# Gates of the first 128 tokens scattered into a table in DRAM and read back by row

## The chip, the core and the metric

One core of a Trainium2 chip. The time is the device time of one execution in microseconds; several runs give a median. One more execution was recorded by the profiler, and its own time stands beside its span.

## The reference

A block with gated, attention and memory branches and a feed-forward is followed by a second block with a state-space mixer, a convolution branch and a layer of experts, all in fp32 for 256 tokens of 1024 features. The change lies in the layer of experts: 16384 experts, numbered (i, j) with i and j below 128. Each token has 8 heads, and each head picks 16 experts with a softmax gate. Cut to that:

```python
q1, q2 = jnp.split(q, 2, axis=-1)                      # 8 heads
s1 = jnp.einsum("thd,hkd->thk", q1, sub_keys_1)
s2 = jnp.einsum("thd,hkd->thk", q2, sub_keys_2)
v1, i1 = lax.top_k(s1, 16); v2, i2 = lax.top_k(s2, 16)
cand = (v1[..., :, None] + v2[..., None, :]).reshape(t, 8, 256)
cand_idx = (i1[..., :, None] * 128 + i2[..., None, :]).reshape(t, 8, 256)
top_s, pos = lax.top_k(cand, 16)
expert_idx = jnp.take_along_axis(cand_idx, pos, axis=-1)
gate = jax.nn.softmax(top_s, axis=-1)
act = gelu(einsum("td,thkd->thk", x, w_down[expert_idx])) * gate
y = einsum("thk,thkd->td", act, w_up[expert_idx])
```

Different heads of one token can pick the same expert; its gates then add.

## The kernel before

The kernel computes every expert for every token and makes the choice a multiplication with a table of gates that is zero nearly everywhere. `AT` holds, on partition j, for each i (128 rows) and each of the 256 tokens, first the activation and then its product with the gate.

Fp32 weights are split into a coarse and a fine fp32r half by `load_split` (lines 210 to 216): SP loads `wf` (four buffers), ScalarE casts it to `wh`, VectorE subtracts to get `wl` (three buffers each). A product is then three matmuls (`mm3`, lines 220 to 222).

In the order of the program:

- First block, with its feed-forward in the loop `for g in range(9)` (weights `w_ff1` and `w_ff2`, matmuls into `ff` and the output banks). GpSimd's queue has one memset and one small operation there.
- Second block's mixer. Then queries (`w_q`) and scores.
- `select(t)`, once for each half of the tokens, finds the experts on VectorE (top 16 in lines 1291 to 1297, positions and softmax to 1338) and leaves i, j and gate in `sl`, token on the partition, one column for each of the 8 x 16 choices. Three transposes (line 1342) and a copy (line 1343) turn them into `jt`, one column a token, a part of the buffer `small`.
- Down projection: loop over pairs of i, 128 weight tiles `wd`, each 24 matmuls into `S` (lines 220 to 222). Gelu brings a pair into `AT` (lines 1440, 1443), and the tokens whose gates are there already are multiplied in on the way (line 1444).
- `gates()`, beside the down projection, in 64 blocks of four tokens: `og` (VectorE, line 1407) is the one-hot of i times the gate, `oh` (ScalarE, lines 1409 and 1410) the one-hot of j, and for each token one product of the two (line 1414) gives the 128x128 table of its gates in `pg`. Rows of `AT` that are there are multiplied by it (line 1418), the others get it as a first value (line 1421).
- Up projection: loop over i. A row of `AT` is split into `ah` (ScalarE, line 346) and `al` (VectorE, line 347), the weights `wu` into `wh` and `wl`, and 12 matmuls add into `acc` (line 1470). `ah` and `al` have two buffers up to row 96 and four after it.
- The end: norm and output.

Selection and gates are generators in a list of background work (`Background`). After each weight tile `bg.run` takes steps from it until the tile's budget is used: `BUDGET["select"]` up to the first block of gates, `BUDGET["down"]` from there. A step's cost is what it yields (a block of gates 1.1 + 0.5).

That is the order in which the program is traced. A planner then orders each engine's queue: among the instructions whose inputs and buffers are ready by its own clock, that which was traced first goes first. Only what is pinned (`pin`) keeps its place. On the chip every queue runs in the order it was given, each instruction waiting for its semaphores; SP's and GpSimd's DMAs too.

Of the kernel before, what the change touches and what calls it, by code (L numbers as in the profile page):

```python
# [7 lines left out]
F32 = mybir.dt.float32  # L8
F32R = mybir.dt.float32r
I32 = mybir.dt.int32  # L10
U32 = mybir.dt.uint32
AF = mybir.ActivationFunctionType
OP = mybir.AluOpType
AX = mybir.AxisListType
PSUM = bass.MemoryType.PSUM

P = 128
T = 256
# [17 lines left out]
for _n, _w in _ROWS:  # L36
# [8 lines left out]
BUDGET = dict(  # L45
    qk=1.5, kv=7.03, u=2.75, wo=2.51, diag=2.05,
    conf_c=0.995, xbc_c=1.4, conv=1.0,
    z=3.3, z_b=0.867, dt_wait=0.0575, ln_wait=6.66, wo2=3.32, wo2_b=5.58, gn_b=0.1,
    q=0.772, q_b=1.27, select=1.21, down=1.87,
)  # L50
FFN_WAIT, MIX_WAIT = 4.5, 5.5

# [104 lines left out]
def tile_two_blocks(ctx: ExitStack, tc: tile.TileContext, A, out):  # L157
    nc = tc.nc
    bg = Background()
# [7 lines left out]
    def bank(name):  # L167
        return ppool.tile([P, 512], F32, tag="bank", name=name)

    cst = cpool.tile([P, NCST], F32, name="cst")  # L170
    ident = cst[:, 0:P]
# [3 lines left out]
    iota = cst[:, 4 * P:5 * P]  # L175
# [9 lines left out]
    rows = cpool.tile([P, NROW], F32, name="rows")  # L185
# [144 lines left out]
    def pin(ins):  # L330
        tc.keep_in_program_order(ins)
# [55 lines left out]
    resid = sres.enter_context(tc.tile_pool(name="resid", bufs=1))  # L387
# [6 lines left out]
    ap = s1a.enter_context(tc.tile_pool(name="ap", bufs=1))  # L394
# [62 lines left out]
    for t in range(2):  # L457
        r = rc1[:, t:t + 1]
# [345 lines left out]
    def activations(g, bs):  # L804
# [7 lines left out]
            split_to(ah[:, 2 * i:2 * i + 2, :], al[:, 2 * i:2 * i + 2, :], a)  # L812
        held.append((ah, al))

    for g in range(9):
        if g < 8:
            bs, outs = pair_banks(4, f"ff1_{g}")
            if g == 0:

                pb = outs2[5][0]  # L820
                ch.add(stats_steps(fp, x1, "ffn", rbf, eps1, where=(outs2[7][0], [pb[:, 0:P], pb[:, P:T]]), wait=FFN_WAIT))
            proj_fm(A["w_ff1"][:, :, g * 512:(g + 1) * 512], 8, 4, h2h, h2l, outs, chain=1.0)
            if g == 0:
                first_bs = bs
                continue
            if g == 1:
                ch.drain()
                activations(0, first_bs)
            activations(g, bs)
        if g == 1:  # L830
            ch.add(meta_steps())
            bg.add(tap_blocks())
        if g >= 1:
            ah, al = held[g - 1]
            for j in range(4):
                k = (g - 1) * 4 + j
                wh, wl = load_split(A["w_ff2"][:, k, :], [P, 1024])
                for m, (o, fb) in enumerate(outs2):
                    c = slice(m * P, (m + 1) * P)
                    mm3(o, wh[:, c], wl[:, c], ah[:, j, :], al[:, j, :], k == 0 and fb, k == 31)  # L840
                ch.run(1.0)
                bg.run(BUDGET["diag"])
# [456 lines left out]

    ready = dict(q=0)  # L1300

    def select(t):
        for h in range(8):
            while ready["q"] < h // 2 + 1:
                yield None
            for s in range(2):
                yield from top16(V[:, h, s, :], Ix[:, h, s, :], sc[t][:, 2 * h + s, :], tk[s])
            cand = cands[h % 2]
            pin(nc.vector.tensor_add(cand, V[:, h, 0, :].unsqueeze(2).to_broadcast([P, 16, 16]),
                                 V[:, h, 1, :].unsqueeze(1).to_broadcast([P, 16, 16])))  # L1310
            yield 0.4
            yield from top16(ts[:, h, :], pos[:, h, :], cand.rearrange("p a b -> p (a b)"), tk2[h % 2])
        while ready["q"] < 8:
            yield None

        pin(nc.vector.tensor_scalar(ab[:, 0], pos, 4, None, op0=OP.logical_shift_right))
        nc.vector.tensor_scalar(ab[:, 1], pos, 15, None, op0=OP.bitwise_and)
        nc.vector.tensor_copy(abf, ab)
        nc.vector.tensor_copy(If, Ix)
        yield 1.0  # L1320
        for s in range(2):
            for q in range(2):
                hs = slice(4 * q, 4 * q + 4)
                e3 = eq.rearrange("p h j a -> p (h j) a")
                pin(nc.vector.tensor_tensor(e3, abf[:, s, hs].rearrange("p h j -> p (h j)").unsqueeze(2).to_broadcast([P, 64, 16]),
                                        iota[:, 0:16].unsqueeze(1).to_broadcast([P, 64, 16]), op=OP.is_equal))
                yield 1.2
                for h in range(4):
                    pin(nc.vector.tensor_mul(eq[:, h], eq[:, h], If[:, 4 * q + h, s, :].unsqueeze(1).to_broadcast([P, 16, 16])))
                    yield 0.4  # L1330
                pin(nc.vector.reduce_sum(sl[:, s, 64 * q:64 * q + 64], e3, axis=AX.X))
                yield 1.2
        g3 = sl[:, 2, :].rearrange("p (h j) -> p h j", h=8)
        nc.vector.tensor_sub(g3, ts, ts[:, :, 0:1].to_broadcast([P, 8, 16]))
        nc.scalar.activation(g3, g3, AF.Exp)
        nc.vector.reduce_sum(zs, g3, axis=AX.X)
        nc.vector.reciprocal(zs, zs)
        nc.vector.tensor_mul(g3, g3, zs.unsqueeze(2).to_broadcast([P, 8, 16]))
        yield 0.8
        pj = bank(f"pj{t}")  # L1340
        for i in range(3):
            nc.tensor.transpose(pj[:, i * P:(i + 1) * P], sl[:, i, :], ident)
        nc.scalar.copy(jt[:, :, t * P:(t + 1) * P], pj[:, :384].rearrange("p (i c) -> p i c", i=3))
        yield 0.2
# [31 lines left out]
    sq1.close()  # L1376
    small = resid.tile([P, 8 * T], F32, name="small", tag="x2")
    jt = small[:, 0:3 * T].rearrange("p (i t) -> p i t", i=3)
    ready["q"] = 8
    stage = [small[:, 3 * T + i * 512:3 * T + (i + 1) * 512] for i in range(2)]  # L1380

# [3 lines left out]
    atp = sat.enter_context(tc.tile_pool(name="atp", bufs=1))  # L1385
    AT0 = atp.tile([P, NA, T], F32, name="AT0")
    parts = [(0, NA, AT0)]
    state = dict(rows=0, toks=0)

    def at_rows(a, b):  # L1390
        for lo, hi, t in parts:
# [4 lines left out]
    NB = 4  # L1396

    def gates():
        t = p1.tile([P, P - NA, T], F32, tag="at1", name="AT1")
        parts.append((NA, P, t))  # L1400
        for b in range(T // NB):
            t0 = b * NB
            oh = gp.tile([P, NB, P], F32, tag="oh", name=f"oh{b}")
            og = gp.tile([P, NB, P], F32, tag="og", name=f"og{b}")
            for i in range(NB):
                c = t0 + i
                nc.vector.tensor_scalar(og[:, i, :], iota, jt[:, 0, c:c + 1], jt[:, 2, c:c + 1], op0=OP.is_equal, op1=OP.mult)  # L1407

                nc.scalar.activation(oh[:, i, :], iota, AF.Abs, scale=-1.0, bias=jt[:, 1, c:c + 1])  # L1409
            nc.scalar.activation(oh, oh, AF.Relu, scale=-1.0, bias=1.0)  # L1410
            yield 1.1
            pg = bank(f"pg{b}").rearrange("p (t i) -> p t i", t=NB)
            for i in range(NB):
                nc.tensor.matmul(pg[:, i, :], oh[:, i, :], og[:, i, :], start=True, stop=True, skip_group_check=True)  # L1414
            n = state["rows"]
            for a, e, r in at_rows(0, n):
                r = r[:, :, t0:t0 + NB]
                nc.vector.tensor_mul(r, r, pg.rearrange("p t i -> p i t")[:, a:e, :])
            for a, e, r in at_rows(n, P):
                r = r[:, :, t0:t0 + NB]  # L1420
                nc.scalar.copy(r, pg.rearrange("p t i -> p i t")[:, a:e, :])
            state["toks"] = t0 + NB
            yield 0.5
# [4 lines left out]
    for i in range(0, P, 2):  # L1428
        S = bank(f"S{i}").rearrange("p (a t) -> p a t", a=2)
        for e in range(2):  # L1430
            wh, wl = load_split(A["wd"][i + e], [P, 8, P])
            for k in range(8):
                mm3(S[:, e, :], wh[:, k, :], wl[:, k, :], xth[:, k, :], xtl[:, k, :], k == 0 and e == 0, k == 7)
            bg.run(BUDGET["select"] if state["toks"] == 0 else BUDGET["down"])
        n = state["toks"]
        rs = list(at_rows(i, i + 2)) if len(parts) > 1 or i < NA else []
        assert len(rs) == 1
        r = rs[0][2]
        if n < T:
            nc.scalar.activation(r[:, :, n:], S[:, :, n:], AF.Gelu)  # L1440
        if n > 0:
            g = stage[(i // 2) % 2].rearrange("p (a t) -> p a t", a=2)
            nc.scalar.activation(g[:, :, :n], S[:, :, :n], AF.Gelu)
            nc.vector.tensor_mul(r[:, :, :n], r[:, :, :n], g[:, :, :n])
        state["rows"] = i + 2
    bg.drain()

# [3 lines left out]
    late = []  # L1451
    up = gp
    pin(nc.scalar.activation(first, first, AF.Sqrt))
    for i in range(P):
        (_, _, r), = list(at_rows(i, i + 1))
        r = r[:, 0, :]
        if i == NA:

            sat.close()
            up = sp.enter_context(tc.tile_pool(name="up", bufs=4))  # L1460
# [126 lines left out]
```

## Time and profile before

| | us |
|---|---|
| median of 3 runs | 1412.07 |
| lowest and highest | 1408.16, 1412.43 |
| the profiled execution's own time | 1407.69 |
| its span | 1406.0 |
| TensorE busy | 1384.8 (98%) |
| VectorE busy | 1013.7 (72%) |
| ScalarE busy | 814.5 (58%) |
| GpSimd busy | 43.0 (3%) |

The span goes from the first to the last instruction; the own time has 1.7 us around it. TensorE's matmuls are pipelined and their recorded ends are modelled, so that what one costs is read from the chain, where the pieces don't overlap, or from a count in a stretch. The granted clock over the span is 0.997 of full speed. Of a GpSimd DMA the trace shows the time that the engine takes to issue it, and separately the time to landing.

### The profile page before, as it was taken

The numbers are of one execution on the slowest core, as the hardware profiler recorded it, in microseconds if no ns is written. First come the engines' busy times: TensorE is split into PE (matmuls) and PEld (weight loads), VectorE is DVE, ScalarE is ACT, GpSimd is POOL, SyncE is SP. The second block draws the span as 40 slices with busy tenths as digits, with TensorE's granted clock in tenths as the row PEclk, the third lists the DMA queues.
The fourth block names the chain that finished last, engine by engine and source line by source line (L and its number), as shares of the span: only waits on it lengthen the run. The fifth ranks groups of instructions, "written<-read, shape, count | busy, mean of one in ns | idle before, by whom it ended". The sixth has DMA issues, their size and how long they took to land.

```text
span 1406.0 us, 26360 instructions
## 1 busy us (share of the span) xinstructions
PE 1384.8 (98%) x10313; PEld 1279.2 (91%) x10313; DVE 1013.7 (72%) x1966; ACT 814.5 (58%) x1431; POOL 43.0 (3%) x64
## 2 busy tenths in 40 slices
PE   9999999999999999999999999999999999999998
PEld 8988999999889899999999999999998888888886
DVE  6886875647557975889799867788875555555654
ACT  6565443435345764645454569999975555555554
POOL 2300000000310000000000000000000000000000
PEclk9999999999999999999999999999999999999999
DMA  8532665654743335446555544444455566656553
GB/s 273 167 91 94 193 194 193 186 175 137 223 137 113 113 121 181 150 150 188 188 180 187 189 165 136 135 136 136 135 172 188 186 188 188 188 192 184 191 185 116
DMA packets 84109, 233.64 MB, mean 166 GB/s; under 512 B 8816, under 2 KB 17904, under 8 KB 83856
## 3 DMA queue, kind: packets, MB, share of 16 engines
q1 hardware_dynamic: 82112, 228.46, 51.4%
q0 software_dynamic: 1296, 2.92, 0.8%
q8 instruction: 81, 1.33, 0.4%
q10 hardware_dynamic: 576, 0.57, 0.1%
q14 instruction: 44, 0.36, 0.1%
HBM read 226.22 MB, written 1.05 MB: 162 GB/s over the span
## 4 chain that ended last, share of the span: by engine, by line
PE 92%; DVE 3%; ACT 2%; DMA 1%; issue 1%; POOL 0%; SPq 0%; ACTq 0%; DVEq 0%
PE acc L1470 25%; PE S L222 9%; PE S L221 9%; PE S L220 9%; PE pg L1414 4%; PE ff L222 4%; PE ff L221 4%; PE ff L220 4%; PE cv L884 2%; PE wo L220 2%; PE wo L222 1%; PE wo L221 1%; PE cf L220 1%; PE q L221 1%; PE cf L222 1%; PE cf L221 1%
## 5 line engine op out<-in xcount | busy, mean ns | idle before, releaser
L216 DVE TENSOR_TENSOR wl<-wf,wh 128x1024 fp32r<-128x1024 f32 (+1 forms) x425 | 515.8, 1215 | 206.1 <-ACT wh L215 205.9
L215 ACT CAST wh<-wf 128x1024 fp32r<-128x1024 f32 (+1 forms) x425 | 441.8, 1040 | 316.1 <-PE S L221 114.6
L220 PE MATMUL S<-xth,wh 128*128 128x256 f32 x1024 | 291.4, 285 | 0.0
L221 PE MATMUL S<-xtl,wh 128*128 128x256 f32 x1024 | 288.4, 282 | 0.0
L222 PE MATMUL S<-xth,wl 128*128 128x256 f32 x1024 | 288.1, 281 | 0.0
L222 PEld LDWEIGHTS S<-xth,wl 128*128 128x128 f32 x1024 | 194.0, 189 | 0.0
L220 PEld LDWEIGHTS S<-xth,wh 128*128 128x128 f32 x1024 | 193.6, 189 | 0.0
L221 PEld LDWEIGHTS S<-xtl,wh 128*128 128x128 f32 x1024 | 192.4, 188 | 0.0
L1470 PE MATMUL acc<-wh,al 128*128 128x512 f32 x512 | 161.4, 395 | 0.0
L1470 PE MATMUL acc<-wl,ah 128*128 128x512 f32 x512 | 161.4, 395 | 0.0
L1470 PE MATMUL acc<-wh,ah 128*128 128x512 f32 x512 | 161.3, 395 | 0.0
L346 ACT CAST ah<-AT 128x256 fp32r<-128x256 f32 x128 | 51.8, 407 | 157.0 <-DVE wl L216 121.1
L1470 PEld LDWEIGHTS acc<-wh,al 128*128 128x128 f32 x512 | 96.0, 187 | 23.5
L1470 PEld LDWEIGHTS acc<-wl,ah 128*128 128x128 f32 x512 | 96.0, 187 | 23.5
L1470 PEld LDWEIGHTS acc<-wh,ah 128*128 128x128 f32 x512 | 95.9, 187 | 23.3
L347 DVE TENSOR_TENSOR al<-AT,ah 128x256 fp32r<-128x256 f32 x128 | 54.1, 425 | 68.7 <-PE acc L1470 67.9
L1409 ACT ACTIVATE oh<-cst,small 128x128 f32<-128x128 f32 x256 | 87.6, 402 | 0.0
L220 PE MATMUL ff<-h2h,wh 128*128 128x256 f32 x256 | 72.0, 282 | 2.3 <-ACT wh L215 2.0
L1407 DVE TENSOR_SCALAR og<-cst,small 128x128 f32<-128x128 f32 x256 | 73.9, 342 | 0.0
L221 PE MATMUL ff<-h2l,wh 128*128 128x256 f32 x256 | 71.6, 280 | 0.1
L222 PE MATMUL ff<-h2h,wl 128*128 128x256 f32 x256 | 70.9, 280 | 0.7 <-DVE wl L216 0.7
L221 PE MATMUL ff<-fal,wh 128*128 128x256 f32 x256 | 71.3, 280 | 0.0
(482 smaller groups left out, 2699.7 us busy)
## 6 DMA issues: line engine op xcount, KB each, us to landing
wf<-in_wd_dram SPq DMA_DIRECT2D x128, 512.0 KB, 3.5
wf<-in_wu_dram SPq DMA_DIRECT2D x128, 512.0 KB, 4.3
wf<-in_w_ff_dram SPq DMA_DIRECT2D x64, 512.0 KB, 3.5
wf<-in_w_out_dram SPq DMA_DIRECT2D x24, 512.0 KB, 3.5
wf<-in_w_conf_dram SPq DMA_DIRECT2D x16, 512.0 KB, 3.9
wf<-in_w_xbc_dram SPq DMA_DIRECT2D x16, 512.0 KB, 3.9
wf<-in_w_q_dram SPq DMA_DIRECT2D x16, 512.0 KB, 3.7
wf<-in_w_fm_dram SPq DMA_DIRECT2D x8, 512.0 KB, 4.7
```

The lines of the kernel that those rows point to most:

```text
L215: nc.scalar.copy(wh[:, :n], wf[:, :n])
L216: nc.vector.tensor_sub(wl[:, :n], wf[:, :n], wh[:, :n])
L220: nc.tensor.matmul(o, lh, rh, start=start, stop=False, skip_group_check=True)
L221: nc.tensor.matmul(o, lh, rl, start=False, stop=False, skip_group_check=True)
L222: nc.tensor.matmul(o, ll, rh, start=False, stop=stop, skip_group_check=True)
L346: nc.scalar.copy(dh, src)
L347: nc.vector.tensor_sub(dl, src, dh)
L884: nc.tensor.matmul(pcv[32 * g:32 * g + 32, i, :], taps[:, m, g, q, :], r4[:, i, g, 4 * q:4 * q + T], start=(i == 0 and q == 0), stop=(q == ...
L1407: nc.vector.tensor_scalar(og[:, i, :], iota, jt[:, 0, c:c + 1], jt[:, 2, c:c + 1], op0=OP.is_equal, op1=OP.mult)
L1409: nc.scalar.activation(oh[:, i, :], iota, AF.Abs, scale=-1.0, bias=jt[:, 1, c:c + 1])
L1414: nc.tensor.matmul(pg[:, i, :], oh[:, i, :], og[:, i, :], start=True, stop=True, skip_group_check=True)
L1470: nc.tensor.matmul(acc[t][f], l[:, c], w[:, f * 512:(f + 1) * 512], start=False, stop=e, skip_group_check=True)
```

## The change

For tokens 0 to 127 the one-hot products go. Instead:

- A table `G0` of 128 x 128 x 128 fp32 (8 MB) in DRAM is cleared by eight GpSimd DMAs from a tile of zeros, traced one by one in the feed-forward loop of the first block.
- `select(0)` ends in `scatter`: three VectorE operations make the address (i x 128 + j) x 128 + token, and for each of the 128 choices one indirect DMA on GpSimd adds 128 gates, one a token, to the table. The sixteen DMAs of a head are declared free of each other; a head's DMAs wait for those of the head before.
- `gates()` treats only tokens 128 to 255 (32 blocks), and the budget of the down projection goes from 1.87 to 1.05.
- In the down projection tokens 0 to 127 get only Gelu; in the up projection SP loads their gates by rows (three rows, then four at a time, into two parts of `small`, the first into the place of `jt`), and VectorE multiplies each row's 128 first tokens before the split.

```diff
@@ -46,7 +46,7 @@
     qk=1.5, kv=7.03, u=2.75, wo=2.51, diag=2.05,
     conf_c=0.995, xbc_c=1.4, conv=1.0,
     z=3.3, z_b=0.867, dt_wait=0.0575, ln_wait=6.66, wo2=3.32, wo2_b=5.58, gn_b=0.1,
-    q=0.772, q_b=1.27, select=1.21, down=1.87,
+    q=0.772, q_b=1.27, select=1.21, down=1.05,
 )
 FFN_WAIT, MIX_WAIT = 4.5, 5.5
 
@@ -812,7 +812,16 @@
             split_to(ah[:, 2 * i:2 * i + 2, :], al[:, 2 * i:2 * i + 2, :], a)
         held.append((ah, al))
 
+
+    G0 = tc.dram_tile([P * P * P, 1], F32, name="G0")
+    G0z = G0.rearrange("(p c n) o -> p c (n o)", p=P, c=8)
+    zg = dg.tile([P, 512], F32, name="zg")
+    nc.gpsimd.memset(zg, 0.0)
+
     for g in range(9):
+        if g >= 1:
+            nc.gpsimd.dma_start(G0z[:, g - 1, :].rearrange("p (a n) -> p a n", a=4),
+                                zg.unsqueeze(1).to_broadcast([P, 4, 512]))
         if g < 8:
             bs, outs = pair_banks(4, f"ff1_{g}")
             if g == 0:
@@ -1299,6 +1308,22 @@
 
     ready = dict(q=0)
 
+    def scatter(sl):
+
+        e, gv = idx.bitcast(F32), gates0
+        nc.vector.scalar_tensor_tensor(e, sl[:, 0, :], float(P), sl[:, 1, :], op0=OP.mult, op1=OP.add)
+        nc.vector.tensor_scalar(idx, e, float(P), tokc, op0=OP.mult, op1=OP.add)
+        nc.vector.tensor_copy(gv, sl[:, 2, :])
+        for h in range(8):
+            key = f"head{h}"
+            for j in range(16):
+                c = 16 * h + j
+                s = nc.gpsimd.indirect_dma_start(
+                    out=G0, out_offset=bass.IndirectOffsetOnAxis(ap=idx[:, c:c + 1], axis=0),
+                    in_=gv[:, c:c + 1], in_offset=None, compute_op=OP.add)
+                tc.declare_no_dep(s.ins, group=key, reason="the experts of a head differ")
+                tc.add_to_no_dep_group(key, s.ins)
+
     def select(t):
         for h in range(8):
             while ready["q"] < h // 2 + 1:
@@ -1337,6 +1362,9 @@
         nc.vector.reciprocal(zs, zs)
         nc.vector.tensor_mul(g3, g3, zs.unsqueeze(2).to_broadcast([P, 8, 16]))
         yield 0.8
+        if t == 0:
+            scatter(sl)
+            return
         pj = bank(f"pj{t}")
         for i in range(3):
             nc.tensor.transpose(pj[:, i * P:(i + 1) * P], sl[:, i, :], ident)
@@ -1376,6 +1404,11 @@
     sq1.close()
     small = resid.tile([P, 8 * T], F32, name="small", tag="x2")
     jt = small[:, 0:3 * T].rearrange("p (i t) -> p i t", i=3)
+    idx = small[:, 7 * T:7 * T + P].bitcast(U32)
+    gates0 = small[:, 7 * T + P:8 * T]
+    tokc = resid.tile([P, 1], F32, name="tokc", tag="tokc")
+    nc.vector.tensor_mul(idx.bitcast(F32), ident, iota)
+    nc.vector.reduce_sum(tokc, idx.bitcast(F32), axis=AX.X)
     ready["q"] = 8
     stage = [small[:, 3 * T + i * 512:3 * T + (i + 1) * 512] for i in range(2)]
 
@@ -1385,7 +1418,7 @@
     atp = sat.enter_context(tc.tile_pool(name="atp", bufs=1))
     AT0 = atp.tile([P, NA, T], F32, name="AT0")
     parts = [(0, NA, AT0)]
-    state = dict(rows=0, toks=0)
+    state = dict(rows=0, toks=P)
 
     def at_rows(a, b):
         for lo, hi, t in parts:
@@ -1398,8 +1431,8 @@
     def gates():
         t = p1.tile([P, P - NA, T], F32, tag="at1", name="AT1")
         parts.append((NA, P, t))
-        for b in range(T // NB):
-            t0 = b * NB
+        for b in range(P // NB):
+            t0 = P + b * NB
             oh = gp.tile([P, NB, P], F32, tag="oh", name=f"oh{b}")
             og = gp.tile([P, NB, P], F32, tag="og", name=f"og{b}")
             for i in range(NB):
@@ -1431,17 +1464,20 @@
             wh, wl = load_split(A["wd"][i + e], [P, 8, P])
             for k in range(8):
                 mm3(S[:, e, :], wh[:, k, :], wl[:, k, :], xth[:, k, :], xtl[:, k, :], k == 0 and e == 0, k == 7)
-            bg.run(BUDGET["select"] if state["toks"] == 0 else BUDGET["down"])
+            bg.run(BUDGET["select"] if state["toks"] == P else BUDGET["down"])
         n = state["toks"]
         rs = list(at_rows(i, i + 2)) if len(parts) > 1 or i < NA else []
         assert len(rs) == 1
         r = rs[0][2]
-        if n < T:
-            nc.scalar.activation(r[:, :, n:], S[:, :, n:], AF.Gelu)
-        if n > 0:
+        if n == P:
+            nc.scalar.activation(r, S, AF.Gelu)
+        else:
+            nc.scalar.activation(r[:, :, :P], S[:, :, :P], AF.Gelu)
+            if n < T:
+                nc.scalar.activation(r[:, :, n:], S[:, :, n:], AF.Gelu)
             g = stage[(i // 2) % 2].rearrange("p (a t) -> p a t", a=2)
-            nc.scalar.activation(g[:, :, :n], S[:, :, :n], AF.Gelu)
-            nc.vector.tensor_mul(r[:, :, :n], r[:, :, :n], g[:, :, :n])
+            nc.scalar.activation(g[:, :, P:n], S[:, :, P:n], AF.Gelu)
+            nc.vector.tensor_mul(r[:, :, P:n], r[:, :, P:n], g[:, :, P:n])
         state["rows"] = i + 2
     bg.drain()
 
@@ -1451,9 +1487,18 @@
     late = []
     up = gp
     pin(nc.scalar.activation(first, first, AF.Sqrt))
+    G0r = G0.rearrange("(i j t) o -> j i (t o)", i=P, j=P)
+
+    gts = {i: small[:, 512 * (i // 4 % 2):512 * (i // 4 % 2) + 512].rearrange("p (a t) -> p a t", a=4)
+           for i in range(3, P, 4)}
+    gts[0] = jt[:, :, 0:P]
     for i in range(P):
         (_, _, r), = list(at_rows(i, i + 1))
         r = r[:, 0, :]
+        if i in gts:
+            n0, gt = i, gts[i][:, :min(P - i, gts[i].shape[1]), :]
+            nc.sync.dma_start(gt, G0r[:, i:i + gt.shape[1], :])
+        nc.vector.tensor_mul(r[:, :P], r[:, :P], gt[:, i - n0, :])
         if i == NA:
 
             sat.close()
```

## Rows read from the trace of the kernel before

**Rows 1.** Page: busy shares of the engines, shares of the chain

```profile
PE 1384.8 (98%) x10313; PEld 1279.2 (91%) x10313; DVE 1013.7 (72%) x1966; ACT 814.5 (58%) x1431; POOL 43.0 (3%) x64
...
PE 92%; DVE 3%; ACT 2%; DMA 1%; issue 1%; POOL 0%; SPq 0%; ACTq 0%; DVEq 0%
```

**Rows 2.** Stretches, all engines: us, busy us (count), granted clock, DMA share, GB/s

```profile
138.00:146.00 8.00, 8.00 (x69) 8.00 (x69) 6.18 (x11) 2.48 (x5) 0.00 (x0) 1.00 0.27 61
146.00:154.00 8.00, 6.33 (x51) 5.93 (x51) 4.84 (x7) 3.72 (x6) 0.00 (x0) 1.00 0.90 313
240.00:260.00 20.00, 20.00 (x173) 20.00 (x172) 12.12 (x13) 8.57 (x9) 0.00 (x0) 1.00 0.59 185
706.00:826.00 120.00, 120.00 (x1017) 120.00 (x1016) 107.07 (x267) 61.36 (x78) 0.00 (x0) 1.00 0.58 185
826.00:1042.00 216.00, 216.00 (x1855) 216.00 (x1855) 176.24 (x431) 197.26 (x516) 0.00 (x0) 1.00 0.43 138
1042.00:1400.00 358.00, 358.00 (x1536) 287.53 (x1534) 210.55 (x258) 187.38 (x263) 0.00 (x0) 1.00 0.58 182
```

**Rows 3.** Chain that ended last, from 820 us: start us, us, what

```profile
825.42 0.33 PE pj L1342 x3
...
828.60 0.89 PE pg L1414 x8
```

**Rows 4.** Instructions of one tile or line: count, ns, first and last start

```profile
L1414 PE MATMUL pg<-og,oh x512: 270/275/275, 828.4 to 1038.9; 128*128 128x128 f32 x171
...
L1342 PE MATMUL pj<-cst,scr x6: 272/273/273, 705.6 to 825.5; 128*128 128x128 f32 x6
...
L1343 ACT COPY small<-pj x2: 467/467/467, 706.7 to 826.3; 128x384 f32<-128x384 f32 x2
```

**Rows 5.** Groups of VectorE, 700 to 826 and 826 to 1042 us

```profile
L1338 DVE TENSOR_TENSOR scr<-scr 128x128 f32<-128x128 f32 x1 | 0.3, 292 | 0.0
...
L1407 DVE TENSOR_SCALAR og<-cst,small 128x128 f32<-128x128 f32 x248 | 71.3, 342 | 0.0
```

**Rows 6.** DMA issues: engine, count, KB each, median us to landing

```profile
r<-h POOLq DMA_DIRECT2D x32, 71.0 KB, 3.3
...
m<-in_memT_dram SPq DMA_DIRECT2D x4, 256.0 KB, 5.4
...
out_dram<-res SPq DMA_DIRECT2D x4, 256.0 KB, 2.2
...
ws<-in_wsT_dram POOLq DMA_DIRECT2D x1, 384.0 KB, 7.0
```

**Rows 7.** Groups of GpSimd: count, busy us, mean ns of one

```profile
L873 POOL DMA_DIRECT2D r<-h x32 | 16.9, 537 | 36.8 <-PE cv L884 29.2 <-DVE sg L913 7.6
...
L602 POOL DMA_DIRECT2D bsb<-in_bs_dram x6 | 3.3, 564 | 0.0
...
L273 POOL TENSOR_TENSOR rc_y<-sd_y,cst 128x4 f32<-128x4 f32 x2 | 2.0, 1009 | 70.8 <-ACT sd_y L271 70.8
...
L273 POOL TENSOR_TENSOR rc_mem<-sd_mem,cst 128x2 f32<-128x2 f32 x1 | 0.7, 695 | 2.9 <-ACT sd_mem L271 2.9
```

**Rows 8.** Timelines of GpSimd and VectorE from 351 us: start us, us

```profile
351.40 8.49 POOL L873 DMA_DIRECT2D r<-h  x16 [7.63 <-DVE sg L913]
...
352.66 1.20 DVE L216 TENSOR_TENSOR wl<-wf,wh 128x1024 fp32r<-128x1024 f32 x1
```

**Rows 9.** Timelines of VectorE and ScalarE in one period of the up projection

```profile
1201.66 0.42 DVE L347 TENSOR_TENSOR al<-AT,ah 128x256 fp32r<-128x256 f32 x1 [0.56 <-PE acc L1470]
1202.67 1.23 DVE L216 TENSOR_TENSOR wl<-wf,wh 128x1024 fp32r<-128x1024 f32 x1 [0.58 <-ACT wh L215]
...
1201.13 0.41 ACT L346 CAST ah<-AT 128x256 fp32r<-128x256 f32 x1 [1.29 <-DVE wl L216]
1201.59 1.05 ACT L215 CAST wh<-wf 128x1024 fp32r<-128x1024 f32 x1
```

**Rows 10.** Timeline of VectorE at 708 us

```profile
708.28 0.33 DVE L1407 TENSOR_SCALAR og<-cst,small 128x128 f32<-128x128 f32 x1
```

## What the change does to the time: the prediction

> **What bounds the kernel now.** I read the page's busy shares first, then the chain that ended last, then a table of stretches by stage. TensorE is busy 98% of the span and makes 92% of the chain [rows 1]. The stretches [rows 2] show it without a gap from 706 to 1400 us at the full granted clock (1.00), through the stages that the change touches: the second selection beside the down projection (to 826), one-hot gates beside it (826 to 1042), up projection (1042 to 1400). VectorE is busy 107.07 of 120 us, 176.24 of 216 and 210.55 of 358 there, and the DMA engines 0.58, 0.43 and 0.58. So TensorE work taken out of these stages shortens the span, as long as nothing else comes last.
>
> **Removed: half of the one-hot products.** In the chain, the eight matmul records of one block of four tokens take 0.89 us [rows 3]. The 512 records [rows 4] are 64 blocks, 57.0 us. Half go: 32 x 0.89 = 28.5 us, all on the path. The three transposes of the first tokens go too, 0.33 us [rows 3]. ScalarE and VectorE lose half of their one-hot work, which lies beside TensorE and is worth nothing itself. Gain: 28.8 us.
>
> **Added: clearing the table.** Eight GpSimd DMAs of 1 MB (8.39 MB, pieces of 2 KB) in the first feed-forward. Two stretches price a piece. From 138 to 146 us only the 992-byte pieces of `raw` move: 0.27 x 16 engines x 8 us = 34.6 us for 61 GB/s x 8 us = 488 KB, 492 pieces, 70 ns each. From 146 to 154 it is 4 KB pieces of weights: 115 us for 2.50 MB, 611 pieces, 188 ns [rows 2]. The line through both, an estimate, is 32 ns plus 0.038 ns a byte: 110 ns for 2 KB, 52 for 512 B, 32 for 4 B. Clearing is 4096 x 110 ns / 16 = 28 us of all engines. The stage draws 185 GB/s at share 0.59 and the engines reach 313 [rows 2], so, spread out, it costs nothing. Nothing in it waits on the loop, however, and the planner puts ready work far ahead (below), so it may come in one burst near 146 us, when loads are catching up and TensorE already misses 1.7 us of 8 [rows 2]. With half of the engines the loads get 157 GB/s of the 185 wanted for 8.39 MB / 157 GB/s = 53 us: 1.5 MB short, 8 us, less what the four `wf` buffers (2 MB) hold. Bounds 0 and 8 us; I take 2.
>
> **Added: the scatter.** 128 indirect DMAs of 128 four-byte pieces on GpSimd, which has nothing else to do then [rows 2]. It can start when the first selection is through: its transposes start at 705.6 us [rows 4], and three small VectorE operations of about 0.29 us [rows 5] make the indices, so about 709. It must end before the up projection reads the table. Without the 28.8 us TensorE gets there at 1013 instead of 1042; the first load of gates takes 2.2 to 5.4 us (256 KB [rows 6]) and the multiply and split about 1 us, so the scatter has until about 1006. Each head's first DMA waits for the previous head's sixteen: seven landings at 3.3 us (the GpSimd DMA of `r` [rows 6]) are 23 us. That leaves (1006 - 709 - 23) / 128 = 2.14 us for each DMA. No row shows an indirect DMA. From below: a plain one takes GpSimd 0.54 to 0.56 us [rows 7]. From above: issue to landing one after another, 3.3 us (7.0 for the slowest GpSimd DMA, `ws` [rows 6]). I take 1.2: the plain DMA, which also writes 128 pieces for `bsb`, plus one of GpSimd's small arithmetic instructions (0.69 to 1.01 us [rows 7]) for fetching 128 offsets, since plain DMAs issued back to back don't wait for each other's landing (16 in 8.49 us [rows 8]). Then it ends at 709 + 154 + 23 = 886 us, 120 us early, hidden behind the down projection. On the DMA engines it is 16384 x 32 ns / 16 = 33 us; if adding makes a piece four times as dear, 131 us over these 300, which with 0.43 to 0.58 just fills them.
>
> **Moved: the budget.** The gates of the other tokens now get 1.05 a tile instead of 1.87: 32 blocks x 1.6 / 1.05 = 49 tiles after the second selection (826.3 us [rows 4]). A tile is 24 matmuls at 120 us / 1017 = 118 ns [rows 2], 2.83 us; with 28.5 us of products this ends at about 993, 20 us before the down projection does. The buffer of the first gate load (the old `jt`) is free then. So the scatter, not the gates, sets this load's time.
>
> **Added: gates in the up projection.** 33 loads on SP's queue ahead of weight loads, 8.39 MB in 512-byte pieces: 16384 x 52 ns / 16 = 53 us over 358, share 0.58 to 0.73, hidden. The second load overwrites rows 0 and 1 of the first and waits for their multiplies; the weight loads behind it wait too. That can cost a period once (0 to 3 us; I take 1). Later loads find their buffer free by the time SP gets there. The 128 multiplies of 128x128 cost VectorE 0.29 us each (its nearest row [rows 5]); per row it is busy 1.23 + 0.42 us of a period of 2.80 [rows 9], so 1.94 with them. The period is TensorE's: 358 us / 128 rows = 2.80, and VectorE waits 0.56 us for `acc` each time [rows 9].
>
> **Sum.** Span 1406.0, own time 1407.69: 1407.69 - 28.8 + 2 + 1 = 1381.9. The median shown, 1412.07, is 4.4 above this execution, so the same sum from the median is 1386. I forecast 1383, in a case of 1375 to 1390.
>
> **Rival 1, the scatter is late (ends slower).** One mechanism: GpSimd's time for each indirect DMA. Up to 2.14 us it is hidden; at 2.37 (the 29 us gone) the change is worth nothing; at 3.3, the landing row, it ends at 709 + 422 + 23 = 1154, 148 us late: 1531. Typical of it is 2.6: 709 + 333 + 23 = 1065, 59 late, 1442. For it: no row shows such an instruction, and the sixteen of a head must land in memory. Against: back-to-back issue at 0.53. Chance 0.17, of which 0.04 stays faster or equal.
>
> **Rival 2, VectorE keeps GpSimd from building descriptors.** If GpSimd worked only while VectorE is idle, it would have 12.9 us to 826 and 39.8 us after it [rows 2], plus the removed one-hots (128 x 0.342 = 43.8 [rows 5]) and about 20 us of the halved table multiplies, less the 29 us by which the stage is shorter: 87 us for 154 us of work. It ends 67 us into an idle up projection instead of 7 before it: 1383 + 60, about 1443. Against it: at 351 us GpSimd issued 16 DMAs in 8.49 us while VectorE ran operations nearly end to end, `wl` at 1.20 [rows 8]. For it: the og operations are of another kind than those, and an indirect DMA also reads its offsets. Chance 0.08. [...]
>
> **Rival 3, crowded DMA engines.** Adding pieces at over four times 32 ns, or the clearing in one burst, starve the weight loads: 5 to 30 us lost, 1388 to 1412. Chance 0.08.
>
> **Rival 4, a ring between VectorE and ScalarE.** If the multiply of the next row stands behind `wl` of this one, then `ah` waits for it, `wh` for `ah`, `wl` for `wh`: 1.23 + 0.29 + 0.03 + 0.46 + 1.08 = 3.09 us a row [rows 5, 9] against 2.80, 37 us in 128 rows: 1420. Against it: the planner fills gaps with whatever is ready; og of the first block ran at 708.28 us between selection steps, 120 us ahead of its products at 828.4 [rows 4, 10], and the multiplies are ready four rows ahead. Chance 0.07.
>
> **How the numbers follow.** Forecast 0.60, rivals 0.17, 0.08, 0.08, 0.07. The range, 1375 to 1425, holds the forecast, rivals 3 and 4 and the near end of rival 1; some 0.18 lie outside. About 0.3% (4 us) is what a measurement can tell from no change. Faster: 0.60, plus 0.07 of rival 3, 0.04 of rivals 1 and 2: 0.71. Same: 0.04. Slower: 0.25.
>
> **What would show it.** TensorE without gaps from 706 us on, 256 records of products, the up projection starting near 1013 + 2 us: right. [...] Gaps in TensorE near 150 us show the clearing. Most likely to be wrong is the 1.2 us.

## The result, and the profile after

The changed kernel takes 1574.02 us (median of 4 runs, 1572.73 to 1575.61) against 1410.53 for the kernel before: 1.1161 times as long, 95% interval 1.1137 to 1.1184. Forecast were 1383 us and a gain. The profiled execution has a span of 1571.0 us, 165.0 more than before.

The page, first its slices of 39 us. The rows are the engines' busy tenths, the granted clock, and the DMA engines' share:

```profile
PE   8997899999999999999900004999999999999998
...
DVE  6875766666478769898800004766676876666665
...
POOL 3201000003100000007888883000000000000000
PEclk9999899999999999999955556999999999999999
DMA  7535766547533364567722223645446876666663
```

In four slices TensorE, VectorE and the weight loads stand still and GpSimd alone works; the granted clock falls to 0.52 (780 to 966 us, in the stretches below). A smaller dent stands in the fourth and fifth slices. The same in stretches (columns as in [rows 2]):

```profile
140.00:150.00 10.00, 9.19 (x79) 9.00 (x78) 4.47 (x10) 1.60 (x3) 3.18 (x5) 1.00 1.02 367
150.00:160.00 10.00, 0.00 (x0) 0.00 (x0) 0.00 (x0) 0.00 (x0) 0.00 (x0) 0.67 1.03 380
160.00:170.00 10.00, 6.02 (x39) 6.02 (x40) 7.18 (x9) 4.88 (x7) 0.00 (x0) 0.65 0.89 319
...
720.00:780.00 60.00, 60.00 (x509) 60.00 (x509) 57.53 (x175) 27.90 (x33) 51.77 (x28) 1.00 0.77 185
780.00:966.00 186.00, 5.77 (x48) 5.57 (x48) 3.00 (x10) 3.19 (x4) 150.40 (x98) 0.52 0.22 4
966.00:1000.00 34.00, 34.00 (x276) 34.00 (x277) 30.71 (x64) 17.35 (x20) 0.00 (x0) 0.95 0.63 192
```

Who waited for whom between 770 and 975 us, longest first (us in total, times, longest):

```profile
ACT wh L215 <- PE S L221: 194.3, 8, 183.8
DVE AT L1501 <- DMA small<-G: 183.0, 1, 183.0
PEld S L222 <- DVE wl L216: 180.4, 1, 180.4
PE S L222 <- DVE wl L216: 180.2, 1, 180.2
```

ScalarE waits for buffers that TensorE holds, TensorE for `wl` of VectorE, VectorE for the load of gates. L1501 is the new multiply of the up projection, of row 0. It stands on VectorE's queue among the steps of the second selection. VectorE's timeline:

```profile
780.59 0.41 DVE L1303 MATCH_REPLACE8 scr<-scr 128x256 f32<-128x256 f32 x1
963.96 0.29 DVE L1501 TENSOR_TENSOR AT<-AT,small 128x128 f32<-128x128 f32 x1 [182.97 <-DMA small<-G]
964.17 0.42 DVE L1304 MAX8 scr<-scr 128x8 f32<-128x256 f32 x1
964.51 1.21 DVE L216 TENSOR_TENSOR wl<-wf,wh 128x1024 fp32r<-128x1024 f32 x1
```

And on SP's queue the load that it waits for stands amid the weights of the down projection. SP's timeline, then its own wait:

```profile
702.37 74.56 SPq L210 DMA_DIRECT2D wf<-in_wd_dram  x27
961.41 0.38 SPq L1500 DMA_DIRECT2D small<-G  x1
961.88 97.83 SPq L210 DMA_DIRECT2D wf<-in_wd_dram  x33
```

```profile
SPq L1500 <- DMA G<-small: 184.4, 1, 184.4
```

Counted in the trace, this load is SP's 288th DMA and the last `wd` load its 364th, 76 places on; 72 of the 128 `wd` loads lie behind it, so it is placed more than half of the down projection too early. On the chip the scatter lasts from 712 to 960 us; the load's place, at 777, fits a planner that believes it done after some 65 (inferred from the place, and tried with half a scatter below). Instructions of the table's tile:

```profile
L1321 POOL DMA_INDIRECT G<-small x128: 1535/1543/2563, 711.9 to 958.5; - x128
```

The places at which TensorE starts its stages give the account. The first matmuls of the mixer (`cf`), the queries (`q`), the down (`S`) and the up projection (`acc`), and the last of `acc`, all as first and last start of a tile's matmuls:

| | before | after | stage, after less before |
|---|---|---|---|
| `cf` | 323.6 | 335.3 | +11.7 (feed-forward and all ahead of it) |
| `q` | 561.2 | 575.0 | +2.1 |
| `S` | 620.3 | 634.5 | +0.4 |
| `acc` | 1041.8 | 1209.3 | +153.3, of which the pause 180.2 |
| last `acc` | 1399.5 | 1564.1 | -2.9 |
| end of the span | 1406.0 | 1571.0 | +0.4 |

The sum is the 165.0 us. One of the down projection's three groups of matmuls, before and after:

```profile
L220 PE MATMUL S<-xth,wh x1024: 278/280/366, 620.3 to 1041.5; 128*128 128x256 f32 x171
```

```profile
L220 PE MATMUL S<-xth,wh x1024: 276/280/415, 634.5 to 1209.0; 128*128 128x256 f32 x171
```

Without its pause the down projection is 26.9 us shorter, close to the 28.8 forecast. So the gain is there, and it is buried under one wait.

### The profile page after: what moved, and what is told of

The parts are those of the page before. It is cut to its first block, busy times and chain, and to the rows that moved or that the text cites. A ratio compares the mean times of both kernels' runs of the same rounds, so it can differ in the third digit from the quotient of the medians.

```text
span 1571.0 us, 25852 instructions
## 1 busy us (share of the span) xinstructions
PE 1350.4 (86%) x10054; PEld 1251.0 (80%) x10054; DVE 982.4 (63%) x1920; ACT 755.3 (48%) x1251; POOL 259.5 (17%) x201
## 4 chain that ended last, share of the span: by engine, by line
PE 71%; POOL 13%; DMA 5%; issue 4%; DVE 4%; ACT 1%; SPq 1%; POOLq 0%; DVEq 0%; ACTq 0%
PE acc L1515 18%; POOL G L1321 13%; PE S L222 6%; PE S L221 6%; PE S L220 6%; PE ff L222 3%; PE ff L221 3%; PE ff L220 3%; DMA small<-G 3%; PE pg L1447 2%; PE cv L893 2%; PE wo L220 1%; PE wo L222 1%; PE wo L221 1%; SPq L766 1%
## 5 line engine op out<-in xcount | busy, mean ns | idle before, releaser
L222 PE MATMUL S<-xth,wl 128*128 128x256 f32 x1024 | 289.0, 282 | 180.2 <-DVE wl L216 180.2
L1321 POOL DMA_INDIRECT G<-small x128 | 209.4, 1636 | 163.3 <-DVE small L1315 124.5
L1501 DVE TENSOR_TENSOR AT<-AT,small 128x128 f32<-128x128 f32 x128 | 31.1, 286 | 215.8 <-DMA small<-G 215.5
L1515 PE MATMUL acc<-wh,ah 128*128 128x512 f32 x512 | 158.1, 389 | 0.0
```

What stands on the lines that cost most here:

```text
L222: nc.tensor.matmul(o, ll, rh, start=False, stop=stop, skip_group_check=True)
L1321: s = nc.gpsimd.indirect_dma_start(out=G0, out_offset=bass.IndirectOffsetOnAxis(ap=idx[:, c:c + 1], axis=0), in_=gv[:, c:c + 1], in_offset ...
L1501: nc.vector.tensor_mul(r[:, :P], r[:, :P], gt[:, i - n0, :])
L1515: nc.tensor.matmul(acc[t][f], l[:, c], w[:, f * 512:(f + 1) * 512], start=False, stop=e, skip_group_check=True)
```

## The experiments

The kernel before was run beside each group: 1411.29 us (median of 7) beside the first four, 1410.68 beside the last four. In the rows shown, line numbers differ by up to five from those of the changed kernel.

**The first load of gates behind the last tile of the down projection.** One edge more; `loads` collects the weight loads.

```diff
+            with ExitStack() as es:
+                if i == 0:
+                    es.enter_context(tc.issue_after(loads[-1].ins))
                 nc.sync.dma_start(gt, G0r[:, i:i + gt.shape[1], :])
```

> The changed kernel with one edge more: the load of the first three rows of gates stands on SP's queue behind the load of the last down-projection tile, where the planner had put it 76 tiles ahead. Theory A (the early place of that load and of its multiply holds SP and VectorE, and with them TensorE, until the scatter has ended): the 180 us pause goes, the scatter (1.85 to 2.3 us a DMA, ending between 950 and 1005 us) is over before the up projection asks for it, and what is left is the gain of 28.8 us less some 13 us for the clearing: about 1395 us, 1385 to 1405. Theory B (the up projection needs the scatter, and that is late wherever the load stands): a pause of over 100 us stays, over 1500 us.

Measured: 1392.48 us, 0.9856 of the kernel before (0.9832 to 0.9879). The pause is gone, theory A holds: with one edge more the same work is 182 us faster and the sign of the change turns. The edge names the load alone; the planner put the three multiplies later with it (the first ran at 1016.4 us), so that the two runs on single queues below are needed to tell them apart. The scatter is done in time:

```profile
L1322 POOL DMA_INDIRECT G<-small x128: 1534/1695/2690, 714.3 to 993.4; - x128
L1504 SPq DMA_DIRECT2D small<-G x33: 327/377/458, 1012.7 to 1118.0; - x33
```

It ends at 995 us, 18 before that load is issued and 35 before the up projection begins (1029.7). Beside it TensorE keeps its pace: the down projection takes 392.7 us (637.0 to 1029.7).

**That, and the clearing spread out.** The eight DMAs on SP's queue, each behind a weight load, in place of GpSimd's.

```diff
-            nc.gpsimd.dma_start(G0z[:, g - 1, :].rearrange("p (a n) -> p a n", a=4),
-                                zg.unsqueeze(1).to_broadcast([P, 4, 512]))
+            with tc.issue_after(loads[-1].ins):
+                nc.sync.dma_start(G0z[:, g - 1, :].rearrange("p (a n) -> p a n", a=4),
+                                  zg.unsqueeze(1).to_broadcast([P, 4, 512]))
```

> As the run with the late load, and the eight clearing DMAs go out on SP's queue, each behind a weight load of the feed-forward, instead of seven in a burst on GpSimd's queue at 138 us. Theory A with the burst as the cause of the pause at 150 to 160 us: that pause goes as well, about 1382 us, 1377 to 1390. If writing 8 MB costs the stage its time however it is spread: within 4 us of the run with the late load.

Measured: 1381.66 us, 0.9785 (0.9767 to 0.9804), as expected, and faster than both kernels. The mixer starts at 323.5 us (before: 323.6), so that in this execution the 8 MB cost the feed-forward nothing when they come one by one. In the kernel that writes instead of adding (below), which clears in the same way, the mixer starts at 326.5 us: 0 to 3 us, then. The down projection, from 623.9 to 1016.7 us, is 392.8 us long against 421.5: 28.7 less, the forecast's 28.8.

**The clearing alone**, in the kernel before, placed as in the change.

```diff
+    G0 = tc.dram_tile([P * P * P, 1], F32, name="G0")
+    G0z = G0.rearrange("(p c n) o -> p c (n o)", p=P, c=8)
+    zg = dg.tile([P, 512], F32, name="zg")
+    nc.gpsimd.memset(zg, 0.0)
     for g in range(9):
+        if g >= 1:
+            nc.gpsimd.dma_start(G0z[:, g - 1, :].rearrange("p (a n) -> p a n", a=4),
+                                zg.unsqueeze(1).to_broadcast([P, 4, 512]))
```

> The kernel before with the clearing of the table added in the place where the change has it, and nothing else of the change (the table is not used). Clearing alone: if the burst on GpSimd's queue is what holds SP's loads at 137 to 156 us, the kernel is 10 to 15 us slower than before, 1421 to 1426 us; if the pause there has another cause (buffers moved by the new tile, another order), under 4 us.

Measured: 1427.28 us, 1.0111 (1.0094 to 1.0128), some 16 us slower, above the 10 to 15 expected. The profiled execution took 1422.07 us, and its mixer starts 14.4 us late (338.0 against 323.6). Timelines of GpSimd in the changed kernel, then of SP before, and of SP in this kernel:

```profile
137.90 5.28 POOL L823 DMA_DIRECT2D G<-zg  x7 [0.30 <-POOL zg L819]
```

```profile
137.04 8.42 SPq L766 DMA_DIRECT2D raw<-in_cols_dram  x16
145.58 32.78 SPq L210 DMA_DIRECT2D wf<-in_w_ff_dram  x15
```

```profile
137.53 19.20 SPq L766 DMA_DIRECT2D raw<-in_cols_dram  x16
156.85 38.70 SPq L210 DMA_DIRECT2D wf<-in_w_ff_dram  x16
```

Seven of the eight go out within 5.3 us. SP then needs 19.2 us instead of 8.4 to issue sixteen small loads, and the next weights are issued 11 us later. TensorE waits 14.3 us in one piece for `wh`:

```profile
PE ff L220 <- ACT wh L215: 14.9, 2, 14.3
```

Before, its longest wait there was 1.4 us. Why SP's issues take longer is not shown: the DMA engines are full in the same 20 us (share 1.02 and 1.03 in the changed kernel, above). And the run with the clearing spread out changed two things, the time of the eight DMAs and their queue; a spread clearing on GpSimd's queue was not run.

**The first load on GpSimd's queue**, behind the scatter, the multiplies where they were.

```diff
-            nc.sync.dma_start(gt, G0r[:, i:i + gt.shape[1], :])
+            (nc.gpsimd if i == 0 else nc.sync).dma_start(gt, G0r[:, i:i + gt.shape[1], :])
```

> The changed kernel with the first load of gates on GpSimd's queue, behind the scatter, so that SP's queue never waits for it; the three multiplies keep their early place on VectorE's queue. If a VectorE instruction in that place is enough to hold TensorE: the pause stays, 1560 to 1580 us, with SP's weight loads issued on up to the four buffers. If the pause came from SP's queue alone (weight loads behind the waiting load): the pause goes, about 1395 us.

Measured: 1579.85 us (one run). The pause stays, 182.0 us, with no gate load on SP's queue until 1184 us:

```profile
DVE AT L1501 <- DMA small<-G: 184.7, 1, 184.7
PEld S L222 <- DVE wl L216: 182.2, 1, 182.2
PE S L222 <- DVE wl L216: 182.0, 1, 182.0
```

A VectorE instruction in that place is enough.

**The first three multiplies late, their load where it was.**

```diff
+        with ExitStack() as es:
+            if i < 3:
+                es.enter_context(tc.issue_after(last_wd.ins))
             nc.vector.tensor_mul(r[:, :P], r[:, :P], gt[:, i - n0, :])
```

(`last_wd` is the subtraction of the last down-projection tile.)

> The changed kernel with the first three multiplies placed behind the last down-projection tile's subtraction on VectorE; the load of their gates keeps its early place on SP's queue. If a waiting load on SP's queue is enough by itself: the weight loads behind it wait, TensorE works off the tiles in the four buffers (about 12 us) and then pauses until the scatter has ended, about 1560 us, 1550 to 1570. If only the multiply's place counts: the pause goes, about 1395 us.

Measured: 1568.05 us (one run). Now it is ScalarE that waits, for weights behind the waiting load:

```profile
ACT wh L216 <- DMA wf<-in_wd_dram: 180.3, 1, 180.3
PEld S L221 <- ACT wh L216: 174.1, 1, 174.1
PE S L221 <- ACT wh L216: 173.8, 1, 173.8
```

So either queue suffices, and the pause is 6 us shorter than in the changed kernel, half of the 12 that I gave the four buffers. Only with both placed late, as in the run with the late load, is TensorE free.

**Half of the scatter**: heads 4 to 7 aren't scattered, so their gates are missing for the first 128 tokens.

```diff
-        for h in range(8):
+        for h in range(4):
             key = f"head{h}"
```

> The changed kernel with the scatter of the first four heads only, 64 indirect DMAs instead of 128 (the gates of the other four heads are left out for the first 128 tokens). The first load of gates stays where the planner puts it, which is now 11 tiles earlier on SP's queue (about 746 us instead of 777). If the pause is the scatter's end less that place: sixteen DMAs beside busy engines, 48 more at 1.85 us, end at about 836, pause about 92 us instead of 182, time about 1484 us, 1470 to 1495. If the pause is something of fixed length that the scatter starts: about 1574 us; if it is the table's reads: also near 1574, as these are the same.

Measured: 1481.46 us (one run), pause 87.8 us; the last DMA of the scatter begins at 835.0 and ends at 836.5:

```profile
L1321 POOL DMA_INDIRECT G<-small x64: 1535/1542/2561, 712.3 to 835.0; - x64
```

```profile
PE S L222 <- DVE wl L216: 87.8, 1, 87.8
```

The pause is what lies between the planner's place of the load and the real end of the scatter. Both go with the number of DMAs. The load's place moved eleven DMAs forward on SP's queue, from 777 us to 746 for 64 indirect DMAs fewer, so the planner counts about 0.5 us for each; on the chip it is 1.84 while VectorE stands still (1.54 and a gap of 0.30).

**Writing in place of adding**, in the kernel with late load and spread clearing; a gate that two heads give to one expert counts once.

```diff
-                    in_=gv[:, c:c + 1], in_offset=None, compute_op=OP.add)
+                    in_=gv[:, c:c + 1], in_offset=None)
```

> As the run with the late load and spread clearing, but the indirect DMAs write their gates instead of adding them (an expert that two heads of a token pick keeps only one gate). If the addition is what makes an indirect DMA dear on GpSimd: 0.6 to 1.0 us each instead of 1.89. If it is the fetching of 128 offsets and the writing of 128 single pieces: 1.8 to 1.95 us, unchanged. The time is that of the run with the addition within 4 us either way, as the scatter is hidden there.

Measured: 1382.95 us (one run), unchanged in time as expected. GpSimd's groups, here and with the addition (count, busy us, mean ns of one):

```profile
L1323 POOL DMA_INDIRECT G<-small x128 | 151.7, 1185 | 163.2 <-DVE small L1317 124.5 <-issue 38.1 <-DMA G<-small 0.6
```

```profile
L1323 POOL DMA_INDIRECT G<-small x128 | 241.9, 1890 | 163.2 <-DVE small L1317 124.5 <-issue 38.4 <-DMA G<-small 0.3
```

Neither expectation is met whole: with the addition a DMA takes GpSimd 0.70 us more in the mean, and 1.19 are left without it. The shortest of each kind take 1.53 and 0.95, so that I put 0.58 of it down to the addition itself, an estimate. The rest is what the mean has over the shortest, 0.36 and 0.23 us; with the addition they are longer beside VectorE (last section).

**The clearing in the mixer**: on SP's queue behind eight loads of the second output projection (the tile of zeros is made there too).

```diff
+            if g >= 8:
+                with tc.issue_after(loads[-1].ins):
+                    nc.sync.dma_start(G0z[:, g - 8, :].rearrange("p (a n) -> p a n", a=4),
+                                      zg.unsqueeze(1).to_broadcast([P, 4, 512]))
```

> As the run with the late load and spread clearing, but the eight clearing DMAs stand on SP's queue behind the first eight loads of the second output projection (from about 480 us on, where the DMA engines move under 125 GB/s), not in the feed-forward. The down projection began 3.6 us later there than before the change; if that is the clearing's traffic at 145 to 160 us, it goes and the time is about 1378 us, 1375 to 1381; if the clearing costs wherever it is, or holds loads in the mixer, 1381 to 1390.

Measured: 1377.87 us, 0.9762 (0.9746 to 0.9778), the fastest of all, but its interval overlaps that of the spread clearing in the feed-forward. And the reason that I gave fell: the down projection starts at 623.0 us, not at 620.3. The loss lies in the mixer, from the first `cf` to the first `q`: 240.8 us in the kernel that clears in the feed-forward and 239.6 in this one, against 237.6 before. So the kernel that doesn't clear there loses more than the one that does. The other kernels with the scatter take 239.2 to 241.3, and the kernel that only clears loses nothing there (338.0 to 575.6). It isn't the table's traffic; what it is stays open.

## Why the prediction was wrong, by its steps

The failed step is the one under "Moved: the budget": "So the scatter, not the gates, sets this load's time." That asks when the load's data is ready, and not where the load stands in its queue. The runs show in its place: the load stood 72 weight tiles ahead of the end of the down projection, waited 184.4 us for the scatter there, and TensorE paused for 180.2 us; placed behind them, load and multiplies cost no pause. No rival of the prediction has such a wait. Two things were wrong in the step.

- The buffer isn't freed by the gates. The first load goes into the part of `jt` for tokens 0 to 127, which nothing uses any more in the changed kernel. So nothing but the scatter held the load back in the planner's clock.
- I had the planner's habit in hand ([rows 10]: an `og` placed 120 us ahead of its products) and used it only where it helps, against rival 4. The same habit puts a load and its multiply ahead as soon as the planner believes the scatter done, and on the chip everything behind them waits for the truth. Of a new wait I priced only who needs its result, not who is queued behind it: on VectorE `wl`, on SP the weights.

The other terms, each beside its measure:

| term | forecast | measured |
|---|---|---|
| half of the products gone | -28.8 us | -28.7 (spread clearing) |
| clearing | +2, bounds 0 to 8 | +11.7 up to the mixer in the changed kernel; alone +14.4 up to there and +16 in the median (1427.28 - 1411.29); 0 to 3 when spread |
| one indirect DMA | 1.2 us | 1.54 and a gap of 0.30 with VectorE idle; 1.89 and 0.30 beside its work |
| heads wait for each other | 23 us | nothing: 127 gaps are 38.8 us, 0.30 each, and the seven waits on the queue take 17 ns each (changed kernel) |
| end of the scatter | 886 us, limit 1006 | 960 in the changed kernel, 982 and 995 without the pause, where the up projection begins at 1017 and 1030 |
| up projection | no loss, or 37 us (rival 4) | 354.8 us against 357.7 |

Rival 1 came nearest in time (1531 at a landing for each DMA) but not by its mechanism: it asked for more than 2.14 us a DMA and a scatter that ends after the down projection. The scatter ended at 960, before the up projection could have begun, and still held TensorE for 180 us. With the load late, 2.19 us a DMA was hidden, above the 2.14 that I allowed, since the seven waits between heads cost nothing.

The clearing was sized wrong because I let the burst compete for bandwidth only. The runs show another price: while it lasts, SP takes 1.2 us to issue a small load in place of 0.5 (19.2 and 8.4 us for sixteen), and the weights stand behind them on that queue. I had seen both, the burst and the sixteen loads, but put them side by side only in GB/s. Whether the full DMA engines make the issue slow, or something in the queues, stays open.

Rival 3 in its second half (the burst) happened, about as dear as I had it there; its first half did not: during the pause 98 of the indirect DMAs filled 0.22 of the DMA engines' time, about 52 ns for each four-byte piece where I had 32 (0.22 x 16 x 186 us / 12544). Rival 4 did not: the multiplies run ahead in VectorE's gaps, as argued. Rival 2 happened in small: GpSimd's DMAs lengthen beside VectorE (1.89 us in the mean against 1.54), and it costs nothing as long as the scatter is hidden. But they are long beside `wl`, not beside `og`, which I had named for it (last section), and that GpSimd builds descriptors in that time is shown by no run. Its sum was also too low: a scatter that ends 67 us after the up projection's start instead of 7 before it is 74 us late, 1457 us and not 1443.

## What to carry to other kernels

A planner that orders queues by its own clock makes a guess at the length of a transfer binding: an instruction that waits for a slow producer belongs, by an explicit edge, behind the work that must not wait for it, on each queue that it passes. When a change adds a wait, look up its entry in every queue and list what stands behind it, before asking whether the data comes in time. And clear or fill memory in pieces tied to the loads that they run beside; here the burst of 7 MB also stretched the issue of the other queue's small loads, from 8.4 to 19.2 us.

## What was unexpected of the hardware

An indirect DMA with addition, of 128 single values, takes GpSimd 1.54 us when VectorE stands still and up to 2.69 beside it. The timelines of GpSimd and VectorE in the kernel with spread clearing show when:

```profile
763.42 1.54 POOL L1323 DMA_INDIRECT G<-small  x1 [0.30 <-issue]
765.27 2.08 POOL L1323 DMA_INDIRECT G<-small  x1 [0.31 <-issue]
767.66 2.40 POOL L1323 DMA_INDIRECT G<-small  x1 [0.30 <-issue]
770.36 1.54 POOL L1323 DMA_INDIRECT G<-small  x1 [0.30 <-issue]
...
832.57 1.54 POOL L1323 DMA_INDIRECT G<-small  x1 [0.30 <-issue]
```

```profile
764.73 1.21 DVE L217 TENSOR_TENSOR wl<-wf,wh 128x1024 fp32r<-128x1024 f32 x1
...
767.43 1.21 DVE L217 TENSOR_TENSOR wl<-wf,wh 128x1024 fp32r<-128x1024 f32 x1
...
770.73 1.21 DVE L217 TENSOR_TENSOR wl<-wf,wh 128x1024 fp32r<-128x1024 f32 x1
...
830.76 2.14 DVE L1442 TENSOR_SCALAR og<-cst,small 128x128 f32<-128x128 f32 x8
```

The DMA that begins at 767.66 falls into a `wl` of 767.43 to 768.64 and is 0.86 us longer; that of 765.27 meets the end of one and is 0.54 longer; that of 770.36, with a `wl` only later, is not. In the first two the added time is what was left of `wl` when the DMA began (0.98 and 0.67 us) less 0.12 to 0.13. VectorE's own time did not change: `wl` takes 1.21 us as elsewhere, also when it begins within a DMA. The longest DMA, of 2.69 us, began 0.06 us before a `wl`. The DMA of 832.57 falls into `og` operations, which have one tensor input, and keeps its 1.54; so, within 0.06 us, do the fourteen that begin while VectorE multiplies rows of `AT` by `pg`, whose second input is in PSUM. What in the DMA waits for `wl` was not tried.

During the pause the granted clock stood at 0.52, and over the 34 us after it at 0.95. The first matmul after it took 0.58 us in place of 0.28; 276 in these 34 us, against 288 at 118 ns each, make 1.4 us, little beside the pause itself.
